# Strassen's product for the sample's input projection, the prompt's projection behind it, and the embedding product first

## The chip, the cores and the metric

The kernel runs on one core of one Trainium2 chip. The metric is the device time of one execution in microseconds. The kernel before took 2343.89 us (median of three runs, 2343.28 to 2348.54).

## The reference, cut to what matters

Two layers of a mixer run over two sequences of 1024 channels: a prompt of 512 tokens and a sample of 1024 tokens. All is float32.

```python
def trunk(x, p, ...):
    h = x
    for i in range(DEPTH):                       # 2
        z = rmsnorm(h, ln1[i]) @ w_in[i]         # 1024 -> 4352 channels
        q, k, v, ga, uf, gf, mga, mgf = jnp.split(z, SPLIT_IDX, axis=-1)
        a = band_attention(rope(q), rope(k), v, sink[i]) * silu(ga)
        f = fourier_mix(uf, w_fmix[i]) * silu(gf)
        merged = sigmoid(mga) * (a @ w_ao[i]) + sigmoid(mgf) * (f @ w_fo[i])
        h = h + merged @ w_out[i]
        gate = sigmoid(rmsnorm(h, ln_pg[i]) @ w_pg[i])
        h = h + (p[i] @ w_pe[i]) * gate
    return rmsnorm(h, ln_f)
```

The prompt and the sample use the same weights.

## The kernel before, in words

**Tiles and chunks.** Activations lie with 128 channels on the partitions and 512 tokens in the free dimension. Chunk 0 is the prompt; chunks 1 and 2 are the sample. A product over 1024 channels goes over 8 k tiles.

**Split products.** Every operand x is split into a high and a low half (`hi_lo`, L77 to L80): ACT writes the rounded copy, VectorE or POOL subtracts it. A product is three matmuls for each k tile: high by high, high by low, low by high (L91, L92, L93). Matmuls of 128x128 by 128x512 are nearly all of TensorE's work.

**One layer.** `project` (L209) makes 34 weight tiles of 128 channels (K, V, four of Q, the gates of attention, the Fourier input, its gates, sixteen merge gates). Each weight tile is loaded and split once (`load_w`, L139: one DMA of 512 KB, one ACT copy, one POOL subtraction) and used for all three chunks. The norm is not applied ahead: `split` (L165) multiplies by the gain only, and the scale by token, which comes from the sums of squares (`Norm`, L172), is put on the results (`scaled`, L227; the rope tables, L245). `finish` (L252) treats each result and stores it to DRAM. `merge` (L301) then makes the branches' projections, the output projection, and the gate of the embedding, and splits the next layer's input chunk by chunk beside the last products.

**What runs beside.** `run` (L695) advances a generator some steps with each step of the projection: the embedding product (`embed`, L422), then attention (`attention`, L455), then the Fourier mixing of both sequences and the first loads of the merge.

**What sets the order.** The program order gives priorities; a list scheduler of the framework sets the queue of each engine, and each engine works its queue in order. All DMAs are issued on SyncE (SP), in order. Buffers rotate: 36 of the tag act, 9 scr, 2 raw weights, 2 split weights (wsp). PSUM has eight banks in four tags (mm, sc, o, misc), two each (L64).

Of the kernel before, what the change touches and what calls it, by code (L numbers as in the profile page):

```python
# [10 lines left out]
F32 = mybir.dt.float32  # L11
# [22 lines left out]
RATE, FOURIER, RATE_F = 1.2, 165, 1.1  # L34
BUFS = dict(act=36, scr=9, raw=2, wsp=2, acc=3, rb=3, tiny=12, stat=20)
# [3 lines left out]
def trunk(ctx: ExitStack, tc: tile.TileContext, x, p, w_in, w_af, w_out, w_pe, w_pg, w_fm,  # L39
# [23 lines left out]
    def pst(tag):  # L63
        return ps.tile([P, T], F32, tag=tag, name=nm(tag), bufs=2)  # L64

    def mm_ps():
        """A bank for the main flow while the other one has none."""
        turn[0] += 1
        return pst(("mm", "sc", "o")[turn[0] % 3])
# [7 lines left out]
    def hi_lo(hi, lo, src, lo_eng):  # L77
        """src = hi + lo exactly, each of 12 bits, which one pass of the tensor engine carries."""
        S.copy(hi, src)  # L79
        lo_eng.tensor_tensor(lo, src, f(hi), op=ALU.subtract)  # L80
# [6 lines left out]
    def mm3_steps(out, ws, xs, each):  # L87
        """out = w.T @ x, of pairs ((w_hi, w_lo), (x_hi, x_lo)), in steps of so many pairs."""
# [50 lines left out]
    def load_w(src, pieces=((KD, G),)):  # L139
        raw = sbt([P, KD, P], F32, "raw")  # L140
        t = sbt([P, 2, KD, P], F32R, "wsp")
        k = 0
        for n, eng in pieces:
            r = slice(k, k + n)
            SY.dma_start(raw[:, r], src[:, r])
            hi_lo(t[:, 0, r], t[:, 1, r], raw[:, r], eng)
            k += n
        return [(t[:, 0, i, :], t[:, 1, i, :]) for i in range(KD)]

# [22 lines left out]
    class Norm:  # L172
# [3 lines left out]
        def add(self, h, eng=G):  # L176
            if self.acc is None:
                self.acc = sbt([P, T], F32, "acc")
# [6 lines left out]
        def stats(self):  # L185
# [5 lines left out]
            # 1 / sqrt(v): a first guess from the exponent, then Newton's steps.  # L191
# [8 lines left out]
        def scale(self):  # L200
# [3 lines left out]
            rb = sbt([P, T], F32, "rb")  # L204
# [4 lines left out]
    def project(l, parts, norms, w):  # L209
        rope_sb, rbs = [], []  # L210

        def rope_tables():
            raws = []
            for pos in (0, T):
                raws.append(big([P, 2, T]))
                SY.dma_start(raws[-1], rope[:, :, pos : pos + T].rearrange("i p t -> p i t"))
            return raws

        def roped(out, c):
            a, b = scr(), scr()  # L220
            V.tensor_tensor(a, out, rope_sb[c][:, 0, :], op=ALU.mult)
            V.stream_shuffle(b, out, [i + 8 if i < 8 else i - 8 if i < 16 else i for i in range(32)])  # L222
            G.tensor_tensor(b, b, rope_sb[c][:, 1, :], op=ALU.mult)
# [3 lines left out]
        def scaled(out, c):  # L227
            a = scr()
            V.tensor_tensor(a, out, rbs[c], op=ALU.mult)  # L229
            return a  # L230

        def transposed(a, c):
# [4 lines left out]
            # Of the first kv head hi | lo, of the second lo | hi.  # L237
# [7 lines left out]
        def scale(c):  # L245
            rbs.append(norms[c].scale())
            t = big([P, 2, T])
            for i in range(2):
                V.tensor_tensor(t[:, i, :], raws[CHUNK_POS[c] // T][:, i, :], rbs[c], op=ALU.mult)
            rope_sb.append(t)  # L250
# [587 lines left out]
```

## Time and profile before

| what | value |
|---|---|
| median of three runs | 2343.89 us |
| the profiled execution's span | 2344.3 us |
| TensorE busy | 2275.7 us, 97% |
| VectorE busy | 1201.6 us, 51% |
| ACT busy | 789.0 us, 34% |
| POOL busy | 658.2 us, 28% |
| HBM traffic | 202.27 MB read, 103.81 MB written |
| matmuls in the projection's first form (L91, mm bank) | 1952, 399 ns each with the pipeline's overlap |

The span is one execution on the hardware profiler; it lies within the range of the runs. In rows of groups the columns are line, engine, operation, output and inputs, shape and count, then busy time, mean ns of one, and the idle time of the engine ahead of them with what ended it. Busy time of a matmul overlaps with its neighbour's, so a matmul's cost is read from the distance of two starts. In rows of the timeline the columns are start, duration, engine, line and operation. VectorE is DVE in these rows.

### The profile page before, as it was taken

The page shows a single profiled execution, that of the slowest core. Times are in us where ns is not written, and L with a number is a line of the kernel's source. Part 1 is how long each engine was busy: PE and PEld are TensorE (multiplying, and loading weights), DVE is VectorE, ACT ScalarE, POOL GpSimd, SP SyncE. Part 2 cuts the span into 40 slices and gives each one's busy share as a digit, 9 for nine tenths or more (in the row PEclk, how much of TensorE's full clock was granted, in tenths as well). Part 3 has the DMA queues.
Part 4 walks back from the last instruction along what each step waited for, and adds up shares of the span by engine and source line. Part 5 has one row for each costly group of instructions (what it writes and reads, how often), then busy time and mean ns, then how long its engine had stood idle before and what let it go on. Part 6 is the DMA issues. An engine that isn't in the chain of part 4 may idle for free. (4 is left out here: it accounts for less than half of the span.)

```text
span 2344.3 us, 29343 instructions
## 1 busy us (share of the span) xinstructions
PE 2275.7 (97%) x10596; PEld 1885.0 (80%) x10596; DVE 1201.6 (51%) x2587; ACT 789.0 (34%) x1594; POOL 658.2 (28%) x427
## 2 busy tenths in 40 slices
PE   7999999999999999999999999999999999999996
PEld 5778887887888888888878788878888888888875
DVE  8532657556454325165574245665554552422767
ACT  5132434444343103143421323344443330212432
POOL 4320111112342333333324011111133323333442
PEclk9999999999999999999999999999999999999997
DMA  4663444433345542214355544444333464322233
GB/s 178 171 198 115 139 138 133 128 116 118 122 148 173 182 135 63 90 61 144 117 148 140 186 126 131 129 137 127 117 108 131 153 220 135 104 77 90 69 124 136
DMA packets 191905, 308.01 MB, mean 131 GB/s; under 512 B 15504, under 2 KB 89360, under 8 KB 191760
## 3 DMA queue, kind: packets, MB, share of 16 engines
q1 hardware_dynamic: 191760, 306.14, 40.5%
q8 instruction: 83, 1.36, 0.2%
q14 instruction: 62, 0.51, 0.1%
HBM read 202.27 MB, written 103.81 MB: 131 GB/s over the span
## 5 line engine op out<-in xcount | busy, mean ns | idle before, releaser
L91 PE MATMUL mm<-act,wsp 128*128 128x512 f32 x1952 | 778.0, 399 | 2.6 <-DVE scr L222 2.6
L92 PE MATMUL mm<-act,wsp 128*128 128x512 f32 x1952 | 763.8, 391 | 1.2 <-DVE act L169 1.2
L93 PE MATMUL mm<-act,wsp 128*128 128x512 f32 x1952 | 763.4, 391 | 0.0
L80 POOL TENSOR_TENSOR wsp<-raw,wsp 128x1024 fp32r<-128x1024 f32 (+2 forms) x125 | 293.6, 2349 | 821.4 <-ACT wsp L79 671.2
L93 PEld LDWEIGHTS mm<-act,wsp 128*128 128x128 f32 x1952 | 366.8, 188 | 78.7
L91 PEld LDWEIGHTS mm<-act,wsp 128*128 128x128 f32 x1952 | 367.7, 188 | 69.9 <-issue 3.0
L92 PEld LDWEIGHTS mm<-act,wsp 128*128 128x128 f32 x1952 | 367.9, 188 | 69.3 <-DVE act L169 2.4
L79 ACT CAST wsp<-raw 128x1024 fp32r<-128x1024 f32 (+2 forms) x134 | 131.5, 986 | 427.0 <-PE mm L93 368.7
L229 DVE TENSOR_TENSOR scr<-mm,rb 128x512 f32<-128x512 f32 x170 | 117.3, 690 | 219.5 <-PE mm L93 218.2
L183 POOL TENSOR_TENSOR acc<-acc,scr 128x512 f32<-128x512 f32 x94 | 128.5, 1367 | 241.7 <-ACT scr L182 236.1
L501 ACT ACTIVATE act<-act,stat 128x384 f32<-128x384 f32 (+1 forms) x192 | 110.0, 574 | 199.4 <-DVE stat L499 198.5
L91 PE MATMUL sc<-act,wsp 128*128 128x512 f32 x416 | 165.9, 399 | 8.5 <-ACT act L168 8.5
L93 PE MATMUL sc<-act,wsp 128*128 128x512 f32 x416 | 165.2, 397 | 2.0 <-POOL wsp L80 2.0
L92 PE MATMUL sc<-act,wsp 128*128 128x512 f32 x416 | 165.7, 398 | 0.0
L91 PE MATMUL o<-act,wsp 128*128 128x512 f32 x416 | 163.2, 392 | 0.0
L92 PE MATMUL o<-act,wsp 128*128 128x512 f32 x416 | 162.6, 391 | 0.2 <-DVE act L169 0.2
L93 PE MATMUL o<-act,wsp 128*128 128x512 f32 x416 | 162.6, 391 | 0.0
L496 DVE CUSTOM_DVE_ANT_0 act<-sc,mask_sb 128x384 f32<-128x384 f32 (+1 forms) x192 | 91.1, 509 | 104.0 <-PE sc L491 103.5
L182 ACT ACTIVATE scr<-act 128x512 f32<-128x512 f32 x105 | 64.4, 628 | 227.6 <-DVE act L341 120.1
L80 DVE TENSOR_TENSOR act<-act,act 128x512 fp32r<-128x512 f32 (+1 forms) x144 | 113.3, 831 | 44.0 <-ACT act L79 40.6
L80 DVE TENSOR_TENSOR act<-misc,act 128x512 fp32r<-128x512 f32 x136 | 90.6, 686 | 52.0 <-ACT act L79 51.4
L323 POOL TENSOR_TENSOR act<-scr,scr 128x512 f32<-128x512 f32 x48 | 64.8, 1351 | 169.4 <-DVE scr L320 169.4
(152 smaller groups left out, 2972.9 us busy)
## 6 DMA issues: line engine op xcount, KB each, us to landing
raw<-in_w_in SPq DMA_DIRECT2D x67, 512.0 KB, 3.6
gt<-scr SPq DMA_DIRECT2D x96, 256.0 KB, 2.0
scr<-gt SPq DMA_DIRECT2D x96, 256.0 KB, 2.8
q<-act SPq DMA_DIRECT2D x48, 256.0 KB, 3.2
gu<-scr SPq DMA_DIRECT2D x48, 256.0 KB, 2.2
pl<-scr SPq DMA_DIRECT2D x48, 256.0 KB, 2.2
act<-q SPq DMA_DIRECT2D x24, 512.0 KB, 5.0
act<-k SPq DMA_DIRECT2D x32, 384.0 KB, 4.1
```

The costliest lines, as they stand in the source:

```text
L79: S.copy(hi, src)
L80: lo_eng.tensor_tensor(lo, src, f(hi), op=ALU.subtract)
L91: PE.matmul(out, wh, xh, start=i == 0, stop=False)
L92: PE.matmul(out, wh, xl, start=False, stop=False)
L93: PE.matmul(out, wl, xh, start=False, stop=i == n - 1)
L182: S.activation(sq, h, AF.Square)
L183: eng.tensor_tensor(self.acc, self.acc, sq, op=ALU.add)
L229: V.tensor_tensor(a, out, rbs[c], op=ALU.mult)
L323: G.tensor_tensor(merged[c][-1][:, m % 2, :], ga, gf, op=ALU.add)
L496: V.tensor_tensor_reduce(out=pr, in0=sc[:, :W], in1=msk, scale=1.0, scalar=-3.0e38, op0=ALU.add, op1=ALU.max, accum_out=mx[:, e])
L501: S.activation(pr, pr, AF.Exp, bias=nmx[:, e], scale=0.125, accum_out=rs[:, e])
```

## The change

Each layer goes in another order, and the sample's projection is made by another algorithm.

1. **Embedding first.** `embed(l)` is the main flow at the beginning of a layer. Beside it the statistics of chunks 1 and 2, their normalisation (`normed`, by VectorE in place), and the parts of the pair product are made.
2. **The pair product.** The sample's two chunks and two weight tiles form a 2 x 2 block product over two halves of the channels. Strassen's scheme in Winograd's form makes it with seven half products instead of eight: each half product is four k tiles, twelve matmuls. Sums of weight halves (S1 to S4) are made on POOL for each pair of weight tiles; sums of activation halves (T1 to T4) are made once per layer, on POOL, and split into high and low. The results are put together on VectorE with one copy on ACT. Attention of the sample runs beside.
3. **The prompt's projection** follows: chunk 0 is loaded again, normalised and split, and its 34 tiles are made with the weights loaded a second time. The Fourier mixing of the sample, the attention of the prompt, the first loads of the merge and the Fourier mixing of the prompt run beside.
4. **Norm ahead.** As the activations are normalised before the split, `finish` no longer scales the results.
5. **Buffers.** act 45, scr 16; the weights use act and not tags of their own. PSUM: mm 3, sc 2, o 2, misc 1.
6. The merge goes over the chunks in the order 1, 2, 0, and no longer splits the next layer's input.

The diff, cut to its core:

```diff
+PS_BUFS = dict(mm=3, sc=2, o=2, misc=1)
...
+    class Pair:
+        ORDER = ("A11", "S2", "S1", "S3", "A12", "A22", "S4")
+        LEAD = 2
...
+        def prepare(self, i):
+            a, name = self.a, self.ORDER[i]
+            if name == "S2":
+                a["S1"], a["S2"] = sbt([P, 4, P], F32, "scr"), sbt([P, 4, P], F32, "scr")
+                G.tensor_tensor(a["S1"], a["A21"], a["A22"], op=ALU.add)
+                G.tensor_tensor(a["S2"], a["S1"], a["A11"], op=ALU.subtract)
+            elif name == "S3":
+                a["S3"] = sbt([P, 4, P], F32, "scr")
+                G.tensor_tensor(a["S3"], a["A11"], a["A21"], op=ALU.subtract)
+            elif name == "S4":
+                a["S4"] = a["S2"]
+                G.tensor_tensor(a["S4"], a["A12"], a["S2"], op=ALU.subtract)
+            t = big([P, 2, 4, P], F32R)
+            hi_lo(t[:, 0], t[:, 1], a[name], V if i % 2 else G)
+            self.w[name] = [(t[:, 0, k, :], t[:, 1, k, :]) for k in range(4)]
...
+            yield from product(0, a, "B11", True)
+            s1 = scr()
+            S.copy(s1, a)
...
+            yield from product(1, b, "T2", True)
+            q = scr()
+            V.tensor_tensor(q, b, s1, op=ALU.add)
...
+    def pair_parts(x, b11, b12, b21, b22):
+        t1, t2 = scr(), scr()
+        x["B11"].append(two(halves(b11, V)))
+        G.tensor_tensor(t1, b12, b11, op=ALU.subtract)
+        G.tensor_tensor(t2, b22, t1, op=ALU.subtract)
+        x["T2"].append(two(halves(t2, V)))
+        x["T1"].append(two(halves(t1, V)))
+        G.tensor_tensor(b12, b22, b12, op=ALU.subtract)
+        x["T3"].append(two(halves(b12, V)))
+        x["B21"].append(two(halves(b21, V)))
+        G.tensor_tensor(b21, b21, t2, op=ALU.subtract)
+        x["T4"].append(two(halves(b21, V)))
+        x["B22"].append(two(halves(b22, V)))
...
-        def scaled(out, c):
-            a = scr()
-            V.tensor_tensor(a, out, rbs[c], op=ALU.mult)
-            return a
...
+    def project_prompt(l, source, rb):
...
+        if rb is None:
+            n = Norm()
+            for k in range(KD):
+                n.add(us[k // 2][:, k % 2, :], V)
+            n.stats()
+            yield
+            rb = n.scale()
...
+            normed(h, k, l, rb)
+            parts.append(two(halves(h, V)))
+        w = load_w(w_in[l, 0])
...
-            if not last:
-                for c in group:
-                    parts[c] = [split(hs[c][k // 2][:, k % 2, :], l + 1, k) for k in range(KD)]
...
-        run(project(l, parts, norms, w), [
-            (embed(l), 4 * NCH * MT_GA, 1.2),
-            (attention(l), 4 * NCH * MT_U, RATE),
-            (chain(fourier(l, 0), fourier(l, 1), start_merge()), 4 * NCH * MT_U + FOURIER, RATE_F),
-        ])
-        parts, norms, w = merge(l, handed.pop())
+        run(embed(l), [(first_pair(xs) if l == 0 else next_pair(xs, l, hs, norm), 2 if l == 0 else 1, 1.0 if l else 0.7)])
+        if l:
+            norm[0].stats()
+            rb = norm[0].scale()
+        w = Pair(w_in[l, 0], w_in[l, 1])
+        for i in range(Pair.LEAD):
+            w.prepare(i)
+        run(project_pair(l, xs, w), [(attention(l, PAIR, True), 14 * 5, 1.33)])
+        prompt = project_prompt(l, x[0] if l == 0 else H[0], rb)
+        while next(prompt) != "made":
+            pass
+        run(prompt, [
+            (fourier(l, 1), 2, 1.7),
+            (chain(attention(l, (0,), False), start_merge(), fourier(l, 0)), 4 * MT_U, 1.8),
+        ])
+        hs, norm = merge(l, handed.pop())
```

Where the engines' queues stand differently, in rows of operation, output and inputs with the program's names:

At the entry of layer 1, VectorE before splits the last chunk's input with the gain alone (L169) and then turns to the tiny operations of the statistics:

```order
L169 SCALAR_TENSOR_TENSOR act1652_9592<-act1416_7980,ln_sb_66,act1652_9592 128x512
L169 SCALAR_TENSOR_TENSOR act1653_9595<-act1441_8179,ln_sb_66,act1653_9595 128x512
L169 SCALAR_TENSOR_TENSOR act1654_9598<-act1441_8179,ln_sb_66,act1654_9598 128x512
L169 SCALAR_TENSOR_TENSOR act1655_9601<-act1466_8378,ln_sb_66,act1655_9601 128x512
L169 SCALAR_TENSOR_TENSOR act1656_9604<-act1466_8378,ln_sb_66,act1656_9604 128x512
L190 TENSOR_SCALAR tiny1663_9646<-misc1662_9641 128x4
```

After the change VectorE's rows at that entry end with the last parts of the pair (L82, of act1666, scr1963, scr1962, act1670, act1720 and act1724) and then the two halves of the embedding's chunk 1, act1975 and act1976:

```order
L82 TENSOR_TENSOR act1964_10447<-act1666_8546,act1964_10447 128x512
L82 TENSOR_TENSOR act1965_10452<-scr1963_10446,act1965_10452 128x512
L82 TENSOR_TENSOR act1966_10455<-scr1962_10445,act1966_10455 128x512
L82 TENSOR_TENSOR act1967_10459<-act1670_8578,act1967_10459 128x512
L82 TENSOR_TENSOR act1968_10462<-act1720_8960,act1968_10462 128x512
L278 TENSOR_SCALAR tiny2013_10671<-misc2012_10666 128x4
```

```order
L82 TENSOR_TENSOR act1969_10466<-act1720_8960,act1969_10466 128x512
L82 TENSOR_TENSOR act1970_10469<-act1724_8992,act1970_10469 128x512
L82 TENSOR_TENSOR act1975_10492<-act1957_10419,act1975_10492 128x512
L82 TENSOR_TENSOR act1976_10495<-act1957_10419,act1976_10495 128x512
L285 SCALAR_TENSOR_TENSOR tiny2014_10672<-tiny2015_10673,tiny2014_10672 128x4
```

The second piece follows the first after seven more tiny operations. The 16 normalisations and the other halves stand ahead of these rows, so the embedding's chunk 1 is behind all of them.

TensorE after the change, from the last pair product of layer 0 (bank mm837) to the prompt's first tile (bank mm883), with the prompt's statistics (L276) and the scale's transposes (L291) between:

```order
L204 MATMUL mm837_4208<-act75_375,act848_4288 128x512 x3
L204 MATMUL mm837_4208<-act90_436,act848_4288 128x512 x3
L204 MATMUL mm837_4208<-act106_499,act848_4288 128x512 x3
L204 MATMUL mm837_4208<-act121_556,act848_4288 128x512 x3
L276 MATMUL misc862_4374<-mean_sb_68,scr854_4351 128x1 x4
L291 MATMUL misc866_4394<-ident_sb_70,tiny864_4380 128x128 x4
L93 MATMUL mm883_4453<-act868_4402,act877_4434 128x512
L94 MATMUL mm883_4453<-act868_4402,act877_4434 128x512
```

Nothing stands between them that does not depend on the prompt's norm. Before the change the three chunks shared each weight tile and there was no such border.

SP after the change at the same place: the four stores of K from the prompt's first tile (act895) stand ahead of the load of its third weight tile (act900):

```order
L744 DMA act886_4470<-in_tab1 128x1024
L744 DMA act887_4471<-in_tab1 128x1024
L373 DMA k0_82<-act895_4509 64x1024 x4
L148 DMA act900_4530<-in_w_in 128x512 x2
L796 DMA scr924_4639<-gu1_89 128x512
```

The load moves to behind stores that wait for the first tile's rope.

More of the change, by code (lines that the diff above doesn't have):

```diff
@@ L31 @@
 NMT = 34
-RATE, FOURIER, RATE_F = 1.2, 165, 1.1
-BUFS = dict(act=36, scr=9, raw=2, wsp=2, acc=3, rb=3, tiny=12, stat=20)
+PAIR = (1, 2)
+ORDER = (1, 2, 0)
+BUFS = dict(act=45, scr=16, tiny=12, stat=20)
+PS_BUFS = dict(mm=3, sc=2, o=2, misc=1)
 @with_exitstack
@@ L203, in scale, with normed @@
                 PE.transpose(rb_ps[:, j * P : (j + 1) * P], r[:, j : j + 1].to_broadcast([P, P]), ident_sb)
-            rb = sbt([P, T], F32, "rb")
+            rb = scr()
             V.tensor_copy(rb, rb_ps)
             return rb
[L209 to L219, printed above, removed]
+    def normed(h, k, gain, rb):
+        V.scalar_tensor_tensor(h, h, ln_sb[:, gain, k : k + 1], rb, op0=ALU.mult, op1=ALU.mult)
@@ L297, in project, with project_pair @@
+            yield from mm3_steps(out, w, parts, 2)
+            tick()
+            p.finish(m, 0, out, False)
+            yield
             w = following
         handed.append(w)
+    def project_pair(l, x, w):
+        p = Projection(l, PAIR)
+        for m in range(0, NMT, 2):
+            steps = w.steps(x, lambda i, j, out, sb: p.finish(m + i, PAIR[j], out, sb),
+                            (lambda: Pair(w_in[l, m + 2], w_in[l, m + 3])) if m + 2 < NMT else None)
+            while True:
+                try:
+                    next(steps)
+                except StopIteration as e:
+                    w = e.value
+                    break
+                tick()
+                yield
@@ L697, in run @@
         n, due = 0, 0.0
-        aux, after, rate = others.pop(0)
+        aux, start, rate = others.pop(0) if others else (iter(()), 0, 0.0)
         for _ in main:
```

273 lines of the change are left out of this document (177 added, 96 removed).

## The prediction, made before the changed kernel ran

> **What bounds the kernel now.** I read the page's head first, then the spacing of the matmuls in the timeline, then the busy time by windows.
>
> ```profile
> span 2344.3 us, 29343 instructions
> PE 2275.7 (97%) x10596; PEld 1885.0 (80%) x10596; DVE 1201.6 (51%) x2587; ACT 789.0 (34%) x1594; POOL 658.2 (28%) x427
> ```
>
> TensorE (PE) is busy 97% of the span, so 2344.3 − 2275.7 = 68.6 us of idle is all that anything beside the matmuls costs today. The span agrees with the median of the runs (2343.89), so every sum is made against 2344.3.
>
> ```profile
> 100.04 0.39 PE L91 MATMUL mm<-act,wsp 128*128 128x512 f32 x1
> 105.48 0.39 PE L91 MATMUL mm<-act,wsp 128*128 128x512 f32 x1
> 22.53 0.63 PE L92 MATMUL sc<-act,wsp 128*128 128x512 f32 x1
> 22.96 0.63 PE L92 MATMUL o<-act,wsp 128*128 128x512 f32 x1
> ```
>
> The first two rows are the same place of two neighbouring tiles, 24 matmuls apart: 5.44 / 24 = 0.2267 us for a 128x512 matmul (the 0.39 holds the pipeline's overlap). The other two, soon after an idle stretch, stand 0.43 us apart: TensorE starts again at about half rate. That lasted six matmuls there, some 1.2 us lost.
>
> ```profile
> 0.00:50.00 50.00, 34.49 (x122) 25.80 (x123) 41.41 (x62) 32.65 (x55) 25.32 (x22) 0.90 0.54 198
> 50.00:100.00 50.00, 45.23 (x213) 37.22 (x212) 32.95 (x65) 8.21 (x13) 17.68 (x11) 1.00 0.56 159
> 800.00:850.00 50.00, 50.00 (x222) 41.39 (x222) 12.94 (x19) 3.16 (x3) 18.65 (x12) 1.00 0.39 127
> 1150.00:1200.00 50.00, 46.34 (x206) 38.00 (x205) 43.26 (x83) 23.76 (x37) 16.40 (x9) 0.93 0.34 107
> 1250.00:1300.00 50.00, 46.56 (x196) 37.77 (x195) 20.50 (x36) 11.08 (x17) 17.49 (x12) 0.95 0.54 153
> ```
>
> The columns are start:end, length, then busy time of PE, weight loads, DVE (VectorE), ACT, POOL, then clock, DMA share, GB/s. Idle is 15.5 + 4.8 = 20.3 us in the first 100 us, 3.7 + 3.4 = 7.1 where layer 1 begins (1150 to 1300), and nothing in mid-projection. Layer 1 begins almost without a stop because the splits of its input (L169) were made beside the last gate products.
>
> **The gain.** In each layer the sample's 34 tiles x 2 chunks x 8 x 3 = 1632 matmuls become 17 pairs x 7 products x 4 x 3 = 1428. That is 204 fewer, 408 in both layers, all 128x512: 408 x 0.2267 = **92.5 us**. They were made on an undisturbed TensorE, so all of it counts: 2344.3 − 92.5 = 2251.8. What matters is how much new idle comes in; the change breaks even at 92.5 us of it.
>
> **The prices of the added work.** The parts need VectorE and POOL at once, which the trace shows to hinder each other.
>
> ```profile
> 1152.38 2.41 POOL L80 TENSOR_TENSOR wsp<-raw,wsp 128x1024 fp32r<-128x1024 f32 x1
> 1153.49 1.85 DVE L356 SCALAR_TENSOR_TENSOR scr<-scr,scr 128x512 f32<-128x512 f32 x1 [2.57 <-DMA scr<-pl]
> 1162.14 0.68 DVE L356 SCALAR_TENSOR_TENSOR scr<-scr,scr 128x512 f32<-128x512 f32 x1
> 23.35 21.31 POOL L183 TENSOR_TENSOR acc<-acc,scr 128x512 f32<-128x512 f32 x14 [3.26 <-ACT scr L182]
> 38.97 8.88 DVE L169 SCALAR_TENSOR_TENSOR act<-act,ln_sb,act 128x512 fp32r<-128x512 f32 x8
> ```
>
> One VectorE operation of two SBUF operands takes 0.68 us alone and 1.85 beside POOL; it ended 0.55 us after POOL's did, as if it had waited for it. Eight of L169 took 1.11 us each while POOL was dense.
>
> ```profile
> L371 DVE SCALAR_TENSOR_TENSOR scr<-act,ln_sb,rb 128x512 f32<-128x512 f32 x18 | 18.5, 1094 | 0.0
> L80 DVE TENSOR_TENSOR act<-act,act 128x512 fp32r<-128x512 f32 x128 | 107.3, 883 | 43.4 <-ACT act L79 40.1 <-DMA pl<-scr 2.9
> L229 DVE TENSOR_TENSOR scr<-mm,rb 128x512 f32<-128x512 f32 x170 | 117.3, 690 | 219.5 <-PE mm L93 218.2
> L183 POOL TENSOR_TENSOR acc<-acc,scr 128x512 f32<-128x512 f32 x94 | 128.5, 1367 | 241.7 <-ACT scr L182 236.1 <-PE misc L188 4.7
> L80 POOL TENSOR_TENSOR act<-act,act 128x512 fp32r<-128x512 f32 x16 | 21.1, 1347 | 19.0 <-ACT act L79 19.0
> L79 ACT CAST act<-act 128x512 fp32r<-128x512 f32 x144 | 80.5, 618 | 41.3 <-POOL act L323 13.7 <-DMA act<-in_w_pe 9.6 <-DVE act L80 6.4
> ```
>
> So I price a normalising operation at 1.09 us, the low half of a split on VectorE at 0.88, both at 0.69 where nothing hinders them (the floor), a POOL operation at 1.37, and the high half on ACT at 0.62. ACT is never the last.
>
> **Start of layer 0: +26.**
>
> ```profile
> GB/s 356 407 356 365 386 363 250 81 331 382 410 407 403 386 391 407 337 87 131 267 382 405 384 407 400 393 368 364 377 393 89 0 0 0 0 0 0 0 19 9
> 1188.55 0.16 DVE L195 SCALAR_TENSOR_TENSOR tiny<-tiny 128x4 f32<-128x4 f32 x1
> 1188.74 0.16 DVE L196 TENSOR_TENSOR tiny<-tiny,tiny 128x4 f32<-128x4 f32 x1
> ```
>
> The first line is the DMA rate from 5 to 40 us in 40 slices: about 380 GB/s. The sample's 4.2 MB behind 1.6 MB of embedding weights and constants is in by 5 + 15 = 20 us. The sums of squares end at about 25; statistics, 24 tiny operations (0.2 apart) and the scale copies bring it to 32. Then VectorE works through 16 normalisations and 21 halves before it reaches the two halves of the embedding's chunk 2, which stand behind them in its order: 16 x 1.09 + 21 x 0.88 + 0.7 + 2 x 0.88 = 38, so 70. The 48 matmuls of that chunk (10.9 us) stand ahead of the pair on TensorE: the pair starts at 81. Until then TensorE has 144 matmuls and the statistics, 35 us: idle 46, against 20.3. With every operation at 0.69 it starts at 71: +16.
>
> **Entry of layer 1: +35.** No L169 work is left beside the gate products; VectorE gets the same parts after the scale is known. From the last gate product to the first normalisation I count 10 us (gate chain, statistics, two Newton sequences). Then come 16 normalisations, 28 halves, 8 tiny operations and a copy ahead of chunk 1's two embedding halves: 16 x 1.09 + 30 x 0.88 + 2.3 = 46, so 56 us after the gate product. Behind them stand 96 embedding matmuls, 21.8 us: 78. TensorE's own work in that time is 36 us: idle 42 against 7.1. Floor: 46 x 0.69 + 2.3 = 34 gives 66 and +23. What is late next is the pair's weights, whose loads stand among the embedding's stores on SP in both layers, but they land while its last matmuls run.
>
> **From pair to prompt: +24 in layer 0, +10 in layer 1.** TensorE's order puts the prompt's statistics right behind the last pair product and its first tile right behind those. In layer 0 that is the last addition (2.5), statistics (1), 12 tiny operations (2.6), transposes and copy (1.5), then 8 normalisations and 8 halves (8 x 1.97 = 15.8, or 11 at the floor); the first tile follows at the pace of its parts, ending 21 us after the pair with 5.4 us of matmuls: 15 idle. Then the load of the third tile's weights stands on SP behind four stores of K, which wait for the rope of the first tile. The load (3.6), its cast and two POOL halves follow, while TensorE has only five short uses of one bank: 9 more. In layer 1 the scale is known and part of the work lies beside the last pair: 10. Floors are 12 and 4.
>
> ```profile
> raw<-in_w_in SPq DMA_DIRECT2D x67, 512.0 KB, 3.6
> L630 ACT COPY scr<-misc 128x256 f32<-128x256 f32 x32 | 11.5, 371 | 15.5 <-PE misc L627 14.4
> L631 DVE TENSOR_TENSOR scr<-scr,misc 128x256 f32<-128x256 f32 x32 | 12.9, 419 | 13.9 <-ACT scr L630 13.1
> L79 ACT CAST act<-misc 128x512 fp32r<-128x512 f32 x136 | 76.8, 579 | 101.7 <-PE misc L527 97.5 <-PE misc L93 4.0
> L80 DVE TENSOR_TENSOR act<-misc,act 128x512 fp32r<-128x512 f32 x136 | 90.6, 686 | 52.0 <-ACT act L79 51.4
> ```
>
> **One misc bank for two: +12.** A bank comes free 0.37 + 0.42 = 0.79 us (256 wide) or 0.58 + 0.69 = 1.27 us (512) after its product. In the prompt's stage the order often puts fewer matmuls than that between two uses; the shortfalls sum to about 13 us a layer, of which half lies in idle already counted. Floor 4.
>
> **Denser pair stage: +18.** A pair of Q tiles is 84 matmuls, 19.0 us. POOL has 4 sums, 4 halves and 4 rope products: 4 x 1.37 + 4 x 1.35 + 4 x 1.37 = 16.4. VectorE has 5 combinations, 12 rope operations and 7 halves: 17 x 0.69 + 7 x 0.88 = 17.9, of which 14 operations read two SBUF operands. If those exclude POOL, the two need 16.4 + 14 x 0.69 = 26.1: 7 over. The 8.88 us row shows less than full exclusion: 8 operations (5.5) and 5.7 us of POOL in it, 11.2 in 8.88; by that ratio 26.1 becomes 20.7. So 2 to 7 for each of four Q pairs in all, I take 3 (12), and 3 a layer for attention beside. The floor is 0, where other pairs' slack takes it in. The ceiling is the row of 1150 to 1200, where DVE is 87% busy and PE loses 3.7 in 50, over 391 us of pair stage: 29 a layer, 58.
>
> [...]
>
> **Half clock after six new gaps: +5**, at 1.2 us less one where a gap only grows; floor 2.
>
> At nothing: the rescaling that goes (L229, 170 operations of VectorE) waited for TensorE, not the reverse; the second load of w_in for the prompt is 512 KB per 5.44 us, 96 GB/s, in a stage like that of 800 to 850, where 127 GB/s cost nothing. The merge keeps its matmuls. An added load that collides would show in the prompt's stage; I give it no more than 5.
>
> Sum: 2251.8 + 26 + 35 + 24 + 10 + 12 + 18 + 5 = **2382 us**, 1.6% slower.
>
> **The rivals.**
> - **VectorE at its undisturbed price (faster).** If ACT paces the parts and POOL's sums fall between VectorE's operations, each costs 0.69: 16 + 23 at the entries, 19 + 8 at the prompt, 12, 0, 5 = 83, which gives 2335; with all floors (16 + 23 + 12 + 4 + 4 + 0 + 2 = 61) 2313. It decides from 85 us of new idle down, that is from a mean of about 0.71 us per operation of the parts. For it: the 0.68 us row, and halves that wait for ACT anyway. Against it: both groups' means, 1.09 and 0.88, come from stages with less POOL work. Chance 0.22.
> - **Break-even.** New idle of 86 to 99, prices halfway: 2337 to 2351. Chance 0.12.
> - **The pair stage is bound by VectorE and POOL.** At the ceiling of 58 for 18 the time is 2422. For it: the 1150 row. Against: only two of a layer's 17 pairs have four ropes. Chance 0.16.
> - That fewer matmuls are not made is excluded: TensorE's order shows the products of four k steps each.
>
> **How the numbers follow.** The forecast has a chance of 0.50. Range: from just above the all-floor sum, 2316, to the ceiling and some collision, 2432. About 0.3% (2336.9 to 2350.9) is what a measurement tells from no change: faster 0.22, same 0.12, slower 0.66.
>
> **What would show it.** Busy PE near 2183 us and some 10190 matmuls prove the gain. Idle of 40 us or more before the pair's first product in both layers, ended by DVE's L82 halves, proves the entries; 20 or less refutes them. PE waiting for L82 and for w_in behind K stores at the prompt proves the third term; waits for `misc` the fourth; idle inside the Q pairs ended by DVE or POOL the fifth. The forecast is wrong most likely in the price of a part: the mean of L298 and of L82 will tell.

## The result, and the profile after

The changed kernel takes 2591.36 us (median of four runs, 2588.47 to 2592.57) against 2343.68: a ratio of 1.1051, with a 95% interval from 1.1035 to 1.1067. It is 10.5% slower. The forecast was 2382, the range ended at 2432: the sign was right, the size far off.

The head of the page, to be set against the first lines of before:

```profile
span 2586.7 us, 30137 instructions
PE 2311.6 (89%) x10188; PEld 1860.1 (72%) x10188; DVE 1385.9 (54%) x2757; ACT 964.0 (37%) x2018; POOL 1090.0 (42%) x833
```

The 408 matmuls are gone (10188 for 10596), yet TensorE is busy 36 us longer, not 92.5 us shorter. Its busy time should be 2275.7 − 92.5 = 2183.2; it is 128 us more, which holds matmuls at half rate (128x512 ones 0.43 us apart from 1850.77 to 1854.18 us, for 0.2267) and the tails of the matmuls ahead of each stop (0.39 us in the records, for 0.2267 from start to start); the two were not told apart. Idle rose from 68.6 to 2586.7 − 2311.6 = 275.1, by 206.5 us. Together −92.5 + 206.5 + 128.4 = 242.4, the whole difference of the two spans. The mean granted clock fell from 0.988 to 0.933.

TensorE's waits (line waited for by the engine, us in total, times, longest):

```profile
PE mm L93 <- ACT act L81: 93.4, 18, 19.7
PE misc L776 <- DVE scr L781: 24.0, 21, 3.2
PE misc L668 <- DVE act L650: 23.8, 26, 1.6
PE mm L204 <- ACT act L81: 22.7, 10, 3.2
PE mm L93 <- ACT scr L590: 20.9, 3, 11.0
PE misc L276 <- DVE scr L271: 10.6, 4, 4.4
PE mm L204 <- DVE act L82: 9.6, 6, 2.8
PE mm L95 <- POOL act L82: 8.2, 11, 1.6
```

L81 and L82 are the halves of a split, L204 the pair product, L590 ACT's copy of an embedding result, L776 the Fourier mixing's products into the one misc bank and L781 VectorE's reading of that bank, L668 the transposes of attention and L650 the softmax scaling ahead of them, L276 and L271 the norm's statistics. L93 to L95 are the products that all other stages share. Before, no such line was above 9.8 us.

By windows, the first layer's pair stage and the prompt's stage (columns as before):

```profile
87.00:533.50 446.50, 415.35 (x1830) 329.80 (x1828) 281.36 (x573) 188.09 (x409) 208.03 (x153) 0.95 0.42 133
533.50:886.00 352.50, 288.10 (x1299) 228.50 (x1300) 172.09 (x452) 147.68 (x350) 148.03 (x125) 0.88 0.48 158
```

The pair stage is idle 31 us and the prompt's 64, in which the clock is 0.88. A stretch at half clock, in the timeline of the second prompt stage:

```profile
1840.63 0.39 PE L776 MATMUL misc<-act,act 128*128 128x256 f32 x1 [1.40 <-DVE act L82]
...
1842.37 0.58 PE L776 MATMUL misc<-act,act 128*128 128x256 f32 x1 [0.92 <-DVE scr L781]
...
1844.40 0.58 PE L776 MATMUL misc<-act,act 128*128 128x256 f32 x1 [0.92 <-DVE scr L781]
...
1849.13 0.77 PE L93 MATMUL mm<-act,act 128*128 128x512 f32 x1
1849.70 0.63 PE L94 MATMUL mm<-act,act 128*128 128x512 f32 x1
```

No wait here is above 1.4 us, but TensorE works only about half of the time (2.5 us of the 5 from 1840 on). From 1842 on the matmuls run at half rate, also the 128x512 ones that follow without a wait (0.43 us apart), up to 1854: the granted clock is 1.00 from 1830 to 1840, 0.60, 0.50 and 0.53 in the next three stretches of 5 us, and 1.00 again from 1855.

### The profile page after: what moved, and what is told of

It reads as the page before. It is cut to its first block, busy times and chain, and to the rows that moved or that the text cites. A ratio compares the mean times of both kernels' runs of the same rounds, so it can differ in the third digit from the quotient of the medians.

```text
span 2586.7 us, 30137 instructions
## 1 busy us (share of the span) xinstructions
PE 2311.6 (89%) x10188; PEld 1860.1 (72%) x10188; DVE 1385.9 (54%) x2757; ACT 964.0 (37%) x2018; POOL 1090.0 (42%) x833
## 5 line engine op out<-in xcount | busy, mean ns | idle before, releaser
L204 PE MATMUL mm<-act,act 128*128 128x512 f32 x2856 | 732.5, 405 | 35.3 <-ACT act L81 22.7
L82 POOL TENSOR_TENSOR act<-act,act 128x512 fp32r<-128x512 f32 x332 | 435.2, 1327 | 572.7 <-ACT act L81 501.7
L204 PEld LDWEIGHTS mm<-act,act 128*128 128x128 f32 x2856 | 549.4, 195 | 155.2 <-ACT act L81 27.2
L93 PE MATMUL mm<-act,act 128*128 128x512 f32 x1132 | 469.8, 415 | 114.4 <-ACT act L81 93.4
L81 ACT CAST act<-act 128x512 fp32r<-128x512 f32 x574 | 327.5, 607 | 460.9 <-DMA act<-in_w_af 163.2
L95 PE MATMUL mm<-act,act 128*128 128x512 f32 x1132 | 464.5, 410 | 9.2 <-POOL act L82 8.2
L94 PE MATMUL mm<-act,act 128*128 128x512 f32 x1132 | 462.9, 409 | 4.0 <-DVE act L82 4.0
L93 PEld LDWEIGHTS mm<-act,act 128*128 128x128 f32 x1132 | 224.8, 199 | 164.2 <-ACT act L81 99.5
L95 PEld LDWEIGHTS mm<-act,act 128*128 128x128 f32 x1132 | 224.0, 198 | 65.5 <-POOL act L82 19.7
L94 PEld LDWEIGHTS mm<-act,act 128*128 128x128 f32 x1132 | 225.6, 199 | 48.4 <-DVE act L82 5.9
L82 DVE TENSOR_TENSOR act<-act,act 128x512 fp32r<-128x512 f32 (+1 forms) x242 | 196.6, 854 | 102.6 <-ACT act L81 101.6
L271 POOL TENSOR_TENSOR scr<-scr,scr 128x512 f32<-128x512 f32 x81 | 106.9, 1322 | 244.8 <-ACT scr L270 227.9
L81 ACT CAST act<-scr 128x512 fp32r<-128x512 f32 (+1 forms) x214 | 124.6, 600 | 165.6 <-DVE scr L343 95.2
L82 DVE TENSOR_TENSOR act<-scr,act 128x512 fp32r<-128x512 f32 (+1 forms) x146 | 125.4, 869 | 78.7 <-ACT act L81 78.0
L82 POOL TENSOR_TENSOR act<-scr,act 128x512 fp32r<-128x512 f32 x68 | 93.7, 1379 | 138.6 <-ACT act L81 86.6
L82 DVE TENSOR_TENSOR act<-misc,act 128x512 fp32r<-128x512 f32 x136 | 93.7, 689 | 102.2 <-ACT act L81 101.9
L95 PE MATMUL o<-act,act 128*128 128x512 f32 (+2 forms) x380 | 145.2, 382 | 2.1 <-DVE act L82 1.9
L93 PE MATMUL o<-act,act 128*128 128x512 f32 (+2 forms) x380 | 145.1, 382 | 1.2 <-ACT act L81 1.2
L94 PE MATMUL o<-act,act 128*128 128x512 f32 (+2 forms) x380 | 145.0, 382 | 0.0
L95 PE MATMUL sc<-act,act 128*128 128x512 f32 (+2 forms) x376 | 143.2, 381 | 1.5 <-DVE act L82 1.4
```

The lines of the kernel that those rows point to most:

```text
L93: PE.matmul(out, wh, xh, start=i == 0, stop=False)
L94: PE.matmul(out, wh, xl, start=False, stop=False)
L95: PE.matmul(out, wl, xh, start=False, stop=i == n - 1)
L204: PE.matmul(bank, w, v, start=first and k == 0 and n == 0, stop=k == 3 and n == 2, skip_group_check=True)
L271: eng.tensor_tensor(self.acc, self.acc, sq, op=ALU.add)
```

## The experiments

Each edit is made in the changed kernel (spans and stage lengths are those of the profiled execution). The pair stages are read from the first to the last row of the pair product: 445.8 us and 445.6 us in the changed kernel.

### Undoing the product alone: the order costs 167 us, Strassen's product 80 more

```diff
-        ORDER = ("A11", "S2", "S1", "S3", "A12", "A22", "S4")
+        ORDER = ("A11", "A12", "A21", "A22")
...
-            yield from product(0, a, "B11", True)
+            for n in range(8):
+                i, j, h = n // 4, n // 2 % 2, n % 2
```

> The sample's pairs of tiles are made by eight plain half products in place of Strassen's seven, in the changed kernel's order: 408 matmuls more (92.5 us), and without the 16 POOL sums and 12 further halves a layer, the four weight sums and three further weight halves a pair, and five combinations a pair. Theory 'the order costs': the prompt's own stage and the entries keep their idle time, and the time is above that of the changed kernel, 2620 to 2690. Rival 'Strassen's vector work costs': without it the pair stages and the entries lose so much idle time that the 92.5 us are outweighed, 2570 or less.

Measured: 2511.11 us, 80 us **faster** than with Strassen's product, although it makes the 408 matmuls again. The pair stage and the prompt's stage of layer 0:

```profile
65.40:501.50 436.10, 436.08 (x2033) 358.93 (x2031) 181.53 (x465) 150.99 (x339) 64.83 (x51) 1.00 0.43 136
501.50:858.00 356.50, 288.95 (x1302) 229.24 (x1303) 175.90 (x456) 151.47 (x357) 149.23 (x125) 0.88 0.48 156
```

By the number this is the rival, but the order has a cost as well. The plain pair stage has no idle time at all, at full clock: 436 us. Strassen's should have been 46 us shorter (204 matmuls), 390, and was 446. So all of the gain and 10 us more was lost inside the stage, in each layer. The pair begins at 65.4 for 87.1 us. The prompt's stage is much the same: 68 us idle of 356, where it was 64 of 352. Against the kernel before, with the same 10596 matmuls, the new order with all that belongs to it (buffers, banks, the norm ahead) costs 2511 − 2344 = 167 us.

### Which part of the product costs: the weight sums, not the combinations

```diff
-                G.tensor_tensor(a["S1"], a["A21"], a["A22"], op=ALU.add)
...
+            if name[0] == "S":
+                a[name] = a[dict(S1="A21", S2="A22", S3="A21", S4="A12")[name]]
```

> Leaves out POOL's four sums of weight halves for each pair of tiles (136 operations of 1.3 us); the products take raw halves in their place. Theory 'weight sums': they hold up POOL's rope products and share VectorE's way to SBUF; without them most of the waits of L204 (about 19 us in each pair stage) and half of those of L668 (12 us in each) go, with the half clock behind them: 35 to 60 us less than the changed kernel, 2530 to 2555. Rival 'combinations': the sums are hidden and VectorE's five combinations a pair cost the time, 12 us less or fewer, 2578 or more.

Measured: 2526.94 us, 64 less. That the sums share a way to SBUF with VectorE, as the theory puts it, is shown neither by this run nor by a later one; what the runs show are times and durations. The transposes' wait for the softmax scaling (L668 for L650 in the changed kernel) fell from 23.8 to 8.8 us; the pair stages are 419.4 and 420.5 us.

```diff
-            V.tensor_tensor(q, c, q, op=ALU.add)
-            finish(0, 1, q, True)
+            finish(0, 1, c, False)
```

> Leaves out the five combinations of the half products a pair (170 operations of VectorE at 0.69 us) and the copy on ACT; the results are finished from the banks as they stand. Theory 'combinations': VectorE has less in the way of the rope, the weight halves and the attention: 35 to 60 us less than the changed kernel, 2530 to 2555. Rival 'weight sums': 12 us less or fewer, 2578 or more. Equal shares of 20 to 30 us in this kernel and in the one without sums would say that the in-order queues are late by the sum of all that stands in them.

Measured: 2587.51 us, 4 less, within what two runs can tell. VectorE's busy time fell by 99 us (1385.9 to 1287.1), and that was worth next to nothing; 136 POOL operations less were worth 64 us. The equal shares did not come.

### Sums because they are on POOL, or because they are work

```diff
-                G.tensor_tensor(a["S1"], a["A21"], a["A22"], op=ALU.add)
+                V.tensor_tensor(a["S1"], a["A21"], a["A22"], op=ALU.add)
... (so for S2, S3 and S4)
```

> The four sums of weight halves of a pair are made by VectorE in place of POOL; all is computed as in the changed kernel. Theory 'POOL beside VectorE': what the sums cost is that POOL holds back VectorE's operations of two SBUF operands and its own rope products; on VectorE they are 136 x 0.69 = 94 us of an engine that has room (the combinations, 117 us, cost nothing there): 35 to 60 us less than the changed kernel, 2530 to 2555. Rival 'work is work': VectorE is as late with the sums as POOL was, or later: 10 us less or fewer, or slower, 2580 or more.

Measured: 2559.22 us (four runs, ratio 1.0907, 1.0889 to 1.0925), 32 less with the same arithmetic. That is half of what leaving the sums out gave.

With the same edit and one more:

```diff
-            hi_lo(t[:, 0], t[:, 1], a[name], V if i % 2 else G)
+            hi_lo(t[:, 0], t[:, 1], a[name], V)
```

> Sums and all low halves of the pair's weights on VectorE (136 more operations of 0.7 us or more in its queue, none of the pair's left to POOL but the rope). Theory 'POOL beside VectorE': with POOL nearly still, VectorE's operations all take about 0.7 us and the time is that of the kernel with the sums alone moved or up to 20 us below it. Rival 'VectorE is full': about 1.9 us a pair more on VectorE than it has room for beside rope and attention, 15 us or more above it.

Measured: 2534.12 us, 57 less, and 25 below the sums alone: with 272 operations added to VectorE the kernel is faster still. The groups of VectorE show why. The softmax scaling (128x384, one tensor and one scalar a partition) before, in the changed kernel, with the sums moved, and with the low halves moved too:

```profile
L509 DVE TENSOR_SCALAR act<-act,stat 128x384 f32<-128x384 f32 x128 | 45.1, 416 | 1.1
```

```profile
L650 DVE TENSOR_SCALAR act<-act,stat 128x384 f32<-128x384 f32 x128 | 74.4, 643 | 1.1
```

```profile
L650 DVE TENSOR_SCALAR act<-act,stat 128x384 f32<-128x384 f32 x128 | 63.4, 558 | 1.1
```

```profile
L650 DVE TENSOR_SCALAR act<-act,stat 128x384 f32<-128x384 f32 x128 | 45.1, 416 | 0.9
```

Mean ns: 416, 643, 558, 416. POOL is busy 208 of the 446 us of the first pair stage in the changed kernel, 120 of 430 with the sums moved, 26 of 414 with the low halves moved too. Operations that read one bank of PSUM and one tile did not change; the first of the combinations, in the changed kernel (686 ns with the low halves moved as well):

```profile
L215 DVE TENSOR_TENSOR scr<-mm,scr 128x512 f32<-128x512 f32 x34 | 23.3, 686 | 11.8 <-PE mm L204 11.5
```

So the sums on POOL slow the scaling that VectorE does beside them (643 ns for 416), and the combinations are not slowed (686 ns in both).

That this is what TensorE gained is seen in its waits. The transposes' wait for the scaling was 23.8 us in the changed kernel and 9.1 with the sums moved; with the low halves moved too it is gone:

```profile
PE misc L668 <- DVE act L650: 0.2, 1, 0.2
```

The waits of L204 for the casts (L81) did not go: 22.7, 18.1 and 20.3 us. The pair stages went from 446 us each to 414.5 and 417.5. Of these 59 us, 30 are idle time, 23.6 of it this wait; 29 are busy time, with the granted clock up from 0.95 to 0.99. So of the 56 us that each lost against 390, about half is POOL beside VectorE. The other half, 25 and 28 us, stays where POOL is nearly still.

The activation sums alone, in `pair_parts`, with the weight sums on POOL as in the changed kernel:

```diff
-        G.tensor_tensor(t1, b12, b11, op=ALU.subtract)
+        V.tensor_tensor(t1, b12, b11, op=ALU.subtract)
... (so for the other three)
```

> The 16 sums of activation halves a layer are made by VectorE in place of POOL; the rest is as in the changed kernel. Theory 'POOL beside VectorE' for the entries: VectorE has 16 x 0.7 = 11 us more, and its 44 other operations fall from about 1.0 to 0.7 us, 13 us: no change within 8 us, 2580 to 2596, but VectorE's mean for normalisation and halves falls. Rival 'chain over two engines': the parts wait at each k for POOL's chain of two sums (2.6 us); on one engine that goes, and each entry is 8 us or more shorter: 2575 or less.

Measured: 2574.30 us, 17 less; the pair starts at 78.2 us for 87.1. The normalisation, in the changed kernel and here:

```profile
L298 DVE SCALAR_TENSOR_TENSOR act<-act,ln_sb,scr 128x512 f32<-128x512 f32 x48 | 49.0, 1061 | 3.2 <-DMA act<-h 3.1
```

```profile
L298 DVE SCALAR_TENSOR_TENSOR act<-act,ln_sb,scr 128x512 f32<-128x512 f32 x48 | 35.6, 765 | 3.1 <-DMA act<-h 3.0
```

VectorE does more and is done sooner. The size lies just inside the rival's band; its chain over two engines and the slowed operations weren't told apart.

### Late weights, one bank, and the queues

```diff
-                    pm = pst("misc")
+                    pm = pst("mm")
... (in three places)
```

> The Fourier mixing's first products write to a bank of tag mm (three banks, one in use by the prompt's tile) in place of the one misc bank. Theory 'one bank': the waits of L776 and L93 for L781 (24.0 + 3.7 us in the changed kernel) go, with about 1 us of half clock behind each group of them: 30 to 40 us less, 2551 to 2561. Rival 'late weights': the same stretches then wait for the weights' halves (L81), 10 us less or fewer, 2580 or more.

Measured: 2571.65 us, 20 less. Most of the misc wait went (L776 for L781: 24.0 to 5.3 us), but L93's waits for casts (L81), the prompt's weights among them, grew by nearly as much (93.4 to 110.8 us). Between the two theories.

```diff
-            following = load_w(w_in[l, m + 1]) if m + 1 < NMT else load_w(w_af[l, 0])
+            following, ahead = ahead, (load_w(w_in[l, m + 2]) if m + 2 < NMT else load_w(w_af[l, 0]) if m + 2 == NMT else None)
```

> The prompt's projection asks for its weights two tiles ahead in place of one. Theory 'late weights': the waits of L93 for L81 in the two prompt stages after their start (19 + 15 us), those of L95 for POOL's L82 (8 us) and the half clock behind some 18 gaps (about 18 us) go: 45 to 60 us less, 2531 to 2546. Rival 'one bank and vector engines': the fillers' own waits remain and take up what is freed, 15 us less or fewer, 2576 or more.

Measured: 2560.24 us (two runs, 2555.09 and 2565.38), 31 less. L776's wait fell too, 24.0 to 12.9 us, with the bank unchanged. Late weights are a real part, but not all that was thought.

```diff
-                if i == 3 and following is not None:
+                if i == 0 and following is not None:
```

> The next pair's two weight tiles are asked for at the first of the seven products in place of the fourth. Theory 'late weights': in the first 100 us of each pair stage the loads stand on SP behind stores of K and Q that wait for the rope; ahead of them, the waits of L204 for L81 and L82 (35 us in all) and the half clock behind them (about 40 in both pair stages) mostly go: 40 to 60 us less, 2531 to 2551. Rival 'VectorE and POOL': the halves themselves are late since both engines are taken by the rope, 10 us less or fewer, 2580 or more.

Measured: 2587.80 us, 4 less: the rival. What stands in the way is seen in the changed kernel at 112 to 118 us, on POOL and on ACT:

```profile
111.81 1.68 POOL L183 TENSOR_TENSOR scr<-act,scr 128x512 f32<-128x512 f32 x1 [2.22 <-DVE act L82]
113.44 1.30 POOL L180 TENSOR_TENSOR scr<-act,act 128x512 f32<-128x512 f32 x1
114.70 1.28 POOL L342 TENSOR_TENSOR scr<-scr,act 128x512 f32<-128x512 f32 x1
```

```profile
116.79 1.66 ACT L81 CAST act<-scr 128x512 fp32r<-128x512 f32 x3 [3.64 <-DVE scr L343]
```

The rope's product (L342) stands behind two weight sums (L183, L180); VectorE's L343 waits for it, ACT's cast of the rope's result waits for L343, and the casts of the next product's weights stand behind that cast in ACT's queue. POOL is not needed for this: in the run with sums and low halves on VectorE, L343 stands behind the same two sums in VectorE's own queue (L180 at 112.66, L183 at 113.25, L343 at 114.96), and the waits of L204 for L81 remain.

With the same edit and one more:

```diff
-        LEAD = 2
+        LEAD = 3
```

> The next pair's weights are asked for at the first product, and the halves of a product's weights are made three products ahead in place of two. Theory 'in-order queues': with the loads early, the casts still stood on ACT behind the casts of the rope's results, which wait for POOL's rope products behind POOL's weight sums; one product more of lead puts them ahead: the waits of L204 for L81 and L82 (about 20 us in each pair stage) mostly go, 25 to 45 us less than the changed kernel, 2545 to 2566. Rival 'no capacity': ACT, VectorE and POOL are as late with a longer lead, 8 us less or fewer, 2580 or more.

Measured: 2568.84 us, 23 less, just short of the 25 expected. The pair stages are 441.4 and 437.3 us: 4 and 8 less, the rest lies elsewhere. The waits of L204 for L81 and L82 fell only from 35.1 to 23.7 us, so the longer lead is not the cure that this theory expected.

```diff
-        raw = load(0)
+        loaded = [load(c) for c in range(NCH)]
...
+        split_p = [[halves(raw[:, k, :], V) for k in range(2)] for raw in loaded]
         for c in range(NCH):
-            ts = [halves(raw[:, k, :], V) for k in range(2)]
```

> All three chunks of the embedding's input are loaded and split ahead of the pair's parts. Theory 'parts': TensorE does the 96 matmuls that stood behind the parts (21.8 us) while VectorE makes the parts, so the pair product begins 10 us (layer 0, where one chunk was behind) and 20 us (layer 1) earlier, less the half clock: 25 to 40 us less, 2551 to 2566. Rival 'other sources': the parts end later since ACT and POOL are the last, and the pair's start moves by less than 5 us a layer, 2580 or more.

Measured: 2584.78 us, 7 less, in the rival's band; the pair starts at 90.3 us for 87.1, and in layer 1 at 1367.2 for 1368.6. The embedding's matmuls got their halves, and then waited for a bank: its copies (the former L590) stand on ACT behind casts of parts. The long wait of each entry, 14 us, has a new owner.

With the same edit and one more:

```diff
-        run(embed(l), [(first_pair(xs) if l == 0 else next_pair(xs, l, hs, norm), 2 if l == 0 else 1, 1.0 if l else 0.7)])
+        run(embed(l), [])
+        for _ in first_pair(xs) if l == 0 else next_pair(xs, l, hs, norm):
+            pass
```

> The embedding's halves are made ahead and its product stands wholly ahead of the pair's parts in the program, so that ACT's copies of its results stand ahead of the casts of the parts. Theory 'in-order queues': the embedding's 144 matmuls run without a stop and the pair begins when the parts are ready: 20 us earlier in layer 1, 0 to 15 in layer 0, and a few us of half clock: 20 to 45 us less, 2545 to 2570. Rival 'capacity': the parts are later by what the embedding took of the engines, and the pair begins less than 5 us earlier, 2580 or more.

Measured: 2631.36 us, 40 **more**: in the rival's band and far beyond what it meant, since the pair starts later, at 113 us in layer 0. There ACT's squares for the norm stand behind the embedding's copies, and the statistics' matmuls come at 59 us for 25; in layer 1 these matmuls stand on TensorE behind the embedding. In both layers the pair waits for the chain norm, scale, parts, and what stood ahead of that chain, on ACT in layer 0 and on TensorE in layer 1, lengthened the entry (113 us for 87 in layer 0).

### Do the gains add, and is the product worth it

> Strassen's product with all three edits that helped: the Fourier mixing in the mm banks (18 to 20 us alone), the prompt's weights two tiles ahead (30), the pair's weights earlier with a lead of three (20). If they act on different waits: 60 to 72 us less than the changed kernel, 2515 to 2530, still 7% above the kernel before. If one wait takes the other's place: 45 us less or fewer, 2545 or more.

Measured: 2528.70 us, 63 less than the changed kernel, where the three gave 20 + 31 + 23 = 74 alone: they act mostly on different waits.

> Plain half products with the two edits that act on the prompt's stage (Fourier mixing in the mm banks, weights two tiles ahead). Theory 'the prompt's own stage': what is left of the new order's cost beside the entries (20 and 12 us idle) sits in that stage, 45 to 50 us of it fall to these two: 2460 to 2470. Rival 'one wait for another': 2490 or more.

Measured: 2470.20 us, at the upper edge of the expected band, 5.2% above before. Of the order's 167 us, 41 were the prompt's late weights and one bank.

> Sums on VectorE together with the three edits of the kernel with all three (2528.7): if the sums' cost and the three edits' waits are different ones, 35 to 50 us below that, 2478 to 2494; if they are the same waits, 2515 or more. Either way above the plain product with two edits' 2470 less the 92.5 us that Strassen's product saves (2378).

Measured: 2490.15 us, 39 below the three edits: the sums' cost is another one than theirs.

> Strassen's product with weight sums, their low halves and the activation sums all on VectorE, and the three edits (Fourier mixing in mm banks, prompt's weights two ahead, pair's weights early with a lead of three). Theory 'POOL beside VectorE' as the main cost of the product, with separate waits for the three edits: below the 2490 of sums on VectorE with the three edits by what the low halves (25) and the activation sums (17) gave: 2440 to 2460, so below the plain product with two edits (2470) though still above the kernel before. Rival 'VectorE is full': 2480 or more.

Measured: 2471.19 us, 11 above the expected band: the plain product's time is reached, not passed.

> As the kernel with POOL cleared, and the low halves of the prompt's and the merge's weights on VectorE too (4 operations of 128x512 a tile for POOL's 2 of 1.3 us each go to 2 of 0.7 on VectorE). Theory 'POOL beside VectorE': the prompt's stage is shorter by its waits for POOL's L82 (9 us) and by faster VectorE operations, 10 to 30 us less than the kernel with POOL cleared. Rival 'VectorE is full' in the prompt's stage (175 of 350 us busy there before this): no less, or more.

Measured: 2452.61 us (two runs, 2448.24 and 2456.98), 19 less. POOL is busy 15% of the span and VectorE 63%.

> Plain half products with the same care: weight halves of the pair, the prompt's and the merge's tiles on VectorE, Fourier mixing in the mm banks, the prompt's weights two tiles ahead. It stands to the kernel with weights on VectorE (2452.6) as plain to Strassen. Theory 'POOL beside VectorE is the main cost of the product': with POOL cleared in both, Strassen's product is ahead by a good part of its 92.5 us of matmuls, so this one takes 2490 or more. Rival 'VectorE's own share': what the product adds to VectorE costs as much as the matmuls save, and this one takes 2440 to 2465.

Measured: 2457.48 us (four runs), the rival: with POOL cleared in both, Strassen's product and the plain one are equal within the uncertainty of the two. The page of the Strassen kernel and of the plain one:

```profile
PE 2228.2 (91%) x10188; PEld 1810.1 (74%) x10188; DVE 1547.7 (63%) x3293; ACT 961.8 (39%) x2018; POOL 369.8 (15%) x297
```

```profile
PE 2299.4 (94%) x10596; PEld 1887.8 (77%) x10596; DVE 1265.6 (52%) x2829; ACT 884.8 (36%) x1874; POOL 361.9 (15%) x297
```

TensorE's 71 us less of busy time come with 62 us more of idle (218 for 156, from spans of 2446.4 and 2455.2). By stages, against the plain kernel: each pair stage is 20 us shorter (416 and 415 us for 436), not 46; the first pair starts 12.6 us later (78.1 for 65.5), the stretch between the two pair stages is 11.7 us longer, and what follows the second 7.2. In the pair stages the largest wait is now that of L204 for a combination (L221):

```profile
PE mm L204 <- DVE scr L221: 14.6, 6, 4.2
```

There TensorE waits for VectorE. No version beat the kernel before; the best, at 2452.61, stands 4.6% above it.

## Why the prediction was wrong, by its steps

- **The gain, 92.5 us: right** as work. 408 matmuls are gone.
- **The entries: right in length, not in every part.** The pair starts at 87 us (81 said) and, in layer 1, 80 us behind the last gate product (78 said; 1368.6 − 1289.1). The row-by-row walk through VectorE's order gave the length, and the normalisation's 1061 ns met the 1.09 us taken. But "ACT is never the last" failed: the long waits are for ACT's casts (13.7 and 19.7 us) and its copies of the embedding's results (9.8 us in two waits, and 11.0), and ACT in its turn waits for POOL's sums again and again (20 us in ten waits in layer 0, 25 in twelve in layer 1). TensorE is idle 38.5 and 33 us, not 46 and 42; the rest of the length is work at a clock of 0.80 and 0.72.
- **From pair to prompt: the mechanism right.** In layer 0 the waits at the border are 2.7 + 2.5 + 11.0 us (15 said) and 4.1 us for the third tile's weights (9 said); in layer 1 7.3 (10 said). A slip in the sum: the terms of the chain in layer 0 add up to 23.4 us, not to the 21 that it ends with. The prompt's first tile ended some 27 us behind the pair, with half its matmuls at half rate (0.43 us apart up to 557 us, 0.23 behind).
- **"Denser pair stage: +18", ceiling 58: the step that failed.** Against the 390 us that its matmuls leave of the plain stage's 436, each stage took 446: 56 us a layer, 112 for 18. Of the 56, 31 are idle time and 25 are busy time beyond the matmuls' own. The step priced the rope and three us for attention, and took its ceiling from a stretch of before in which POOL was busy a third of the time. It took the slowed operations to be those with two tensors in SBUF; the attention's one-tensor scaling, 416 ns before, took 643, and attention's transposes wait for it: 11.7 of the 31 us of idle, the largest wait of the stage. The upper end of its own 2 to 7 us for a Q pair would have given 4 x 7 + 6 = 34 for this term, on the right side of 18, but for the rope alone. Leaving out the POOL sums gave back 64 us, moving them and the low halves to VectorE 57, all of it in the pair stages. So POOL beside VectorE is shown for about half of the 112. The other half stays with POOL 6% busy; TensorE then waits for casts, halves and combinations, and which order of the queues would free them was not tried.
- **"One misc bank: +12" and what the prompt's stage loses beyond its start: mis-sized.** I costed weights only for the third tile. In SP's order most later loads stand right behind a store as well, and TensorE's later waits there for casts (L93 for L81) are 17.6 us in layer 0, where the third tile's 4.1 is one of five, and 14.9 in layer 1; asking one tile earlier gave 31 us, the bank 20. The order as a whole, with the plain product, costs 167 us; the entries, the border, the bank and the clock were to cost 112, the product's share in the entries included.
- **"Half clock: +5": mis-sized.** Busy time holds 128 us beyond the matmuls' own, tails included. The count of six gaps was far too low: the list of TensorE's waits has 154 for 34 before, and behind waits of about a microsecond, close together, the granted clock was as low (0.50 from 1842 to 1854 us) as behind the one wait of 19.7 us at layer 1's entry (0.50 from 1340 to 1345 us, 0.55 from 1345 to 1350).
- The rival "the pair stage is bound by VectorE and POOL" (2422, chance 0.16) named the right mechanism at half its size. Its objection, that only two of 17 pairs have four ropes, missed that attention runs beside the other pairs.

Open: what would win back the 113 us of the plain product in the new order (2457 against 2344). By the two spans 87 of them are idle time and 24 longer busy time, and of the 156 us of idle 62 and 37 lie in the stretches of the two prompt stages (501 to 850 and 1724 to 2070 us), none in the pair stages. Open as well: why each pair stage of Strassen's product still loses 25 us or more with POOL cleared, where VectorE's order is the likeliest cause and was not tried; and by how much half clock alone lengthens the kernel, which no run took away.

## What to carry to other kernels

Fewer matmuls did not help here: with 408 less the kernel took 2591 us, with the plain product 2511, and in the pair stages every wait of TensorE is for ACT, VectorE or POOL. So price an algorithm's additions at the contended duration of everything that runs beside them (643 ns for 416 in the scaling), not only of the operations added. Work that POOL did "for free" was dearer here than the same work on a busier VectorE (the weight sums: 2591 us on POOL, 2559 on VectorE). A fused stage that covers its neighbours' latencies is an asset: split into a dense stage and a thin one, the plain dense stage had no idle time here, and the thin one 68 us in 356.

## What the hardware showed beyond expectation

- A one-tensor scaling of 128x384 on VectorE went from 416 to 643 ns beside a busy POOL (208 of 446 us of a pair stage), and back to 416 with POOL nearly still (26 of 414), while an operation with one operand in PSUM stayed at 686 to 690 ns.
- Behind waits of 1.27 and 1.40 us, and among and behind four of 0.92 us with about a microsecond of work between, matmuls ran at half rate for some twelve microseconds (1842 to 1854 us: granted clock 0.50, 128x512 matmuls 0.43 us apart), though none of the waits was long.
- VectorE's total busy time rose by only 5 us (1457.2 to 1462.0) when 136 further operations of 128x512 moved to it from POOL, with the other 136 already there.
